# Feature sums by one wide product of ones, in place of token columns and diagonals

## The chip, the core and the metric

The kernel runs on one core of a Trainium2 chip. The metric is the device time of one execution, in microseconds (us). A core has five engines that run their own instruction streams in program order: PE (TensorE, matrix products), DVE (VectorE), ACT (ScalarE), POOL (GpSimd) and SP (SyncE, which only starts transfers here). They wait for each other through semaphores. In profile rows an instruction is given with the line of the kernel that issued it, as L256, and with the tiles it writes and reads, as `mm<-xH,wH`.

## What is computed

Two layers of three sub-layers each act on 512 tokens of 1024 features in float32: a gated feed-forward block (FFN), a mixing block (Mix) and a second FFN. Each sub-layer takes `rmsnorm(x)` over the features, computes its branch, and adds `rmsnorm(branch)` to `x`. Mix holds four branches; one of them, the convolution, ends in a layernorm over 256 features.

```
def rmsnorm(x, g):
    y = x * lax.rsqrt(jnp.mean(x * x, axis=-1, keepdims=True) + EPS)
    return y * g
...
for l in range(DEPTH):
    x = x + 0.5 * rmsnorm(swiglu_ffn(rmsnorm(x, ffn1_pre_g[l]), ...), ffn1_post_g[l])
    x = x + rmsnorm(mixing_sublayer(rmsnorm(x, mix_pre_g[l]), ...), mix_post_g[l])
    x = x + 0.5 * rmsnorm(swiglu_ffn(rmsnorm(x, ffn2_pre_g[l]), ...), ffn2_post_g[l])
```

## The kernel before

Features lie on the 128 partitions and tokens along the row: `x` is 8 tiles of 128x512. Every weight block of 128x1024 is loaded by a transfer (`raw`) and split into a rounded high part `wH` (ACT, L200) and a rest `wL` (DVE, L205, or in places ACT L202 and a transfer that adds on POOL's queue, L203). The activations are split likewise into `xH` (ACT L411) and `xL` (DVE L417). A product is then three matmuls, high by high, high by low and low by high (L256; L290 in the interleaved form `heads`), so PE issues some eleven thousand matmuls. Its results go to 8 banks of the accumulator memory, named by the pools `mm`, `at` and `st`; `st` has two banks.

Two kinds of statistics are on the change's path. They are sums over features, that is over partitions, so PE forms them.

**Before a sub-layer** (`pre_stats`): DVE adds up the squares of `x` (L460) into `sqx`. `compact` multiplies each 128-token block of `sqx` with one column of ones (L317: the block is the stationary operand, the result is one column of tokens), four columns for 512 tokens. DVE takes the inverse square root on this 128x4 tile by small operations without a table (`rsqrt`, L297 to L304), and `diag` (L325) spreads each column over a diagonal 128x128 block. Later `spread` (L333) multiplies ones with the diagonals, which puts each token's value on every partition, and ACT copies it to `rb_` (L365). The sub-layer's products run on unnormalised `x`, since the scale per token can be applied to the result; so only what reads a finished bank (L476 in an FFN, L649 in a Mix) waits for `rb_`.

**After a sub-layer** (`post_stats`, `post_steps`): the same for the branch's output in two token halves of 256 (`lo`, `hi`). The last four of the eight output tiles are computed half by half (`tail`), the statistics of one half run under other products, then for each `k` of 8 DVE scales the output tile (L403, which reads the `spread` bank), DVE or POOL adds it to `x` (L406), ACT makes the next `xH` (L411) and DVE `xL` (L417). The next sub-layer's first four banks (`head`) follow, first for `lo`, then for `hi`; they eat `xH` in the order of `k`. Their end is the compact for the next `pre_stats`, and two more products (`ahead`) come before the first finished bank is needed again.

In Mix the branches are generators that `pump` advances in turn while PE works on gate products; a `yield` gives a cost in ns, and a second number the rounds to sit out. The convolution's layernorm uses compact, diag and spread twice (mean, then variance).

The place of a piece among PE's instructions is set by `after(ns, fn)`, which runs `fn` when an estimate of PE's time has moved on by `ns`:

```
self.after(5600, lambda: nc.scalar.activation(self.rb_, self.spread(dg, FULL), AF.Copy))
...
self.after(3400, lambda: self.step(steps))
```

## Time and profile before

| what | value |
|---|---|
| time, median of 3 runs (lowest to highest) | 2317.3 us (2317.05 to 2317.96) |
| the profiled execution: time, span | 2318.88 us, 2317.2 us |
| PE busy | 2279.9 us, 98% |
| DVE busy | 1195.5 us, 52% |
| ACT busy | 924.4 us, 40% |
| POOL busy | 249.1 us, 11% |

The span reaches from the first to the last instruction of one profiled execution; 1.7 us lie around it. Shares are averages over the whole span, in which long stretches of back-to-back matmuls alternate with the passages from one sub-layer to the next, where DVE, ACT and POOL have a chain of work to finish.

### The profile page before, as it was taken

The numbers are of one execution on the slowest core, as the hardware profiler recorded it, in microseconds if no ns is written. First come the engines' busy times: TensorE is split into PE (matmuls) and PEld (weight loads), VectorE is DVE, ScalarE is ACT, GpSimd is POOL, SyncE is SP. The second block draws the span as 40 slices with busy tenths as digits, with TensorE's granted clock in tenths as the row PEclk, the third lists the DMA queues.
The fourth block names the chain that finished last, engine by engine and source line by source line (L and its number), as shares of the span: only waits on it lengthen the run. The fifth ranks groups of instructions, "written<-read, shape, count | busy, mean of one in ns | idle before, by whom it ended". The sixth has DMA issues, their size and how long they took to land.

```text
span 2317.2 us, 28269 instructions
## 1 busy us (share of the span) xinstructions
PE 2279.9 (98%) x11158; PEld 1907.1 (82%) x11158; DVE 1195.5 (52%) x2144; ACT 924.4 (40%) x1350; POOL 249.1 (11%) x291
## 2 busy tenths in 40 slices
PE   8999999999999999999999999999999999999997
PEld 7888889777888988888888888888787889888886
DVE  5333337799533652434563333478984337424345
ACT  5232224565554532222442222365645545322221
POOL 0000002311431200000100000023123212000001
PEclk9999999999999999999999999999999999999999
DMA  5333333767878432332333333357677774333322
GB/s 171 98 101 92 108 92 99 182 146 168 188 164 184 110 109 91 98 101 90 107 105 97 105 95 102 91 131 162 147 173 162 180 164 109 101 93 94 103 89 69
DMA packets 82557, 282.27 MB, mean 122 GB/s; under 512 B 9428, under 2 KB 13176, under 8 KB 82424
## 3 DMA queue, kind: packets, MB, share of 16 engines
q1 hardware_dynamic: 64136, 213.87, 29.3%
q0 software_dynamic: 18288, 66.59, 16.7%
q8 instruction: 87, 1.43, 0.2%
q14 instruction: 46, 0.38, 0.0%
HBM read 278.32 MB, written 2.10 MB: 121 GB/s over the span
## 4 chain that ended last, share of the span: by engine, by line
PE 87%; DVE 8%; ACT 2%; issue 2%; DMA 1%; POOL 0%; SPq 0%; POOLq 0%; DVEq 0%; ACTq 0%
PE mm L256 49%; PE at L256 31%; DVE ca L868 3%; PE mm L290 2%; PE at L290 2%; DMA wL<-in_w_in_dram 1%; DVE m L937 1%; DVE sc L938 1%; PE st L333 1%; PE st L317 1%; ACT wH L200 1%; ACT wL L202 1%; ACT xH L411 0%; DVE t L649 0%; DVE t L403 0%
## 5 line engine op out<-in xcount | busy, mean ns | idle before, releaser
L200 ACT ACTIVATE wH<-raw 128x1024 fp32r<-128x1024 f32 (+1 forms) x394 | 407.6, 1037 | 828.0 <-issue 570.2
L256 PE MATMUL mm<-xH,wH 128*128 128x512 f32 x1344 | 532.0, 397 | 0.9 <-DVE t L759 0.9
L256 PE MATMUL mm<-xH,wL 128*128 128x512 f32 x1344 | 526.6, 393 | 3.2 <-DMA wL<-in_w_in_dram 3.2
L205 DVE TENSOR_TENSOR wL<-raw,wH 128x1024 fp32r<-128x1024 f32 (+1 forms) x272 | 324.3, 1194 | 247.3 <-ACT wH L200 247.2
L256 PE MATMUL mm<-h,wH 128*128 128x512 f32 (+1 forms) x1496 | 409.1, 354 | 0.0
L256 PE MATMUL mm<-xL,wH 128*128 128x512 f32 x1344 | 359.0, 389 | 0.0
L256 PEld LDWEIGHTS mm<-xH,wL 128*128 128x128 f32 x1344 | 254.2, 189 | 58.5 <-DMA wL<-in_w_in_dram 5.4
L256 PEld LDWEIGHTS mm<-xH,wH 128*128 128x128 f32 x1344 | 254.1, 189 | 57.8 <-issue 5.0
L256 PEld LDWEIGHTS mm<-h,wH 128*128 128x128 f32 x1496 | 263.8, 188 | 41.3
L256 PEld LDWEIGHTS mm<-xL,wH 128*128 128x128 f32 x1344 | 252.3, 188 | 52.5
L256 PE MATMUL at<-xH,wH 128*128 128x512 f32 x704 | 277.4, 396 | 7.3 <-ACT xH L226 6.8
L256 PE MATMUL at<-xH,wL 128*128 128x512 f32 x704 | 274.1, 391 | 0.0
L256 PE MATMUL mm<-h,wL 128*128 128x512 f32 (+1 forms) x748 | 252.4, 352 | 0.0
L256 PE MATMUL at<-h,wH 128*128 128x512 f32 (+1 forms) x776 | 219.6, 366 | 0.0
L202 ACT ACTIVATE wL<-raw 128x1024 fp32r<-128x1024 f32 x122 | 128.4, 1054 | 185.9 <-PE mm L256 129.8
L256 PE MATMUL at<-xL,wH 128*128 128x512 f32 x704 | 187.8, 389 | 0.0
L256 PEld LDWEIGHTS at<-xH,wH 128*128 128x128 f32 x704 | 132.9, 189 | 37.7 <-ACT xH L226 7.1
L256 PEld LDWEIGHTS at<-h,wH 128*128 128x128 f32 x776 | 140.4, 188 | 24.6
L256 PEld LDWEIGHTS mm<-h,wL 128*128 128x128 f32 x748 | 140.4, 188 | 20.3
L256 PEld LDWEIGHTS at<-xH,wL 128*128 128x128 f32 x704 | 132.9, 189 | 29.4 <-issue 1.4
L256 PEld LDWEIGHTS at<-xL,wH 128*128 128x128 f32 x704 | 132.2, 188 | 27.4
L256 PE MATMUL at<-h,wL 128*128 128x512 f32 (+1 forms) x388 | 136.5, 366 | 0.0
(212 smaller groups left out, 2263.4 us busy)
## 6 DMA issues: line engine op xcount, KB each, us to landing
raw<-in_ffn_w_gu_dram SPq DMA_DIRECT2D x173, 512.0 KB, 3.6
raw<-in_w_in_dram SPq DMA_DIRECT2D x98, 512.0 KB, 6.4
wL<-in_w_in_dram POOLq DMA_DIRECT2D x94, 512.0 KB, 7.1
raw<-in_ffn_w_down_dram SPq DMA_DIRECT2D x64, 448.0 KB, 3.3
raw<-in_ffn_w_down_dram SPq DMA_DIRECT2D x32, 512.0 KB, 3.5
raw<-in_w_branch_dram SPq DMA_DIRECT2D x16, 512.0 KB, 5.6
wL<-in_w_branch_dram POOLq DMA_DIRECT2D x16, 512.0 KB, 6.8
raw<-in_w_out_dram SPq DMA_DIRECT2D x16, 512.0 KB, 6.4
```

The costliest lines, as they stand in the source:

```text
L200: self.pin(nc.scalar.activation(h[:, :n], raw[:, :n], AF.Copy))
L202: self.pin(nc.scalar.activation(lo[:, :n], raw[:, :n], AF.Copy, scale=-1.0))
L205: self.pin(nc.vector.tensor_tensor(lo[:, :n], raw[:, :n], h.bitcast(F32)[:, :n], op=ALU.subtract))
L256: self.nc.tensor.matmul(out, w[a], m[b], start=(first and i == 0), stop=(last and i == 3 * n - 1))
L290: self.nc.tensor.matmul(out, w[a], m[b], start=(count[j] == 1), stop=(count[j] == 3 * KD))
L317: self.nc.tensor.matmul(ps[:, c - c0:c - c0 + 1], s[:, c * P:(c + 1) * P], self.ones[:, 0:1], start=(i == 0), stop=(i == len(tiles) - 1))
L333: self.nc.tensor.matmul(ps[:, s], self.ones, dg[:, s], start=True, stop=True)
L868: nc.vector.scalar_tensor_tensor(a, hp[:, t:t + N], dw(t), a, op0=ALU.mult, op1=ALU.add)
L937: nc.vector.max(m8, sc[:, :W])
L938: nc.vector.match_replace(out=sc[:, :W], in_to_replace=m8, in_values=sc[:, :W], imm_value=GONE)
```

## The change

`compact`, `diag` and `spread` go. In their place `sums` multiplies a full 128x128 tile of ones with the squares themselves (L313): one float32 matmul of 512 or 256 columns, whose result holds the token's sum on every partition at once. `rsqrt` then works on 128x512 or 128x256 tiles rather than 128x4 or 128x2, and its result is used from SBUF as it stands; ACT's copy to `rb_` is gone. `ROOT` folds a constant factor into the first operation. In `pre_stats` the sums now stand 2000 ns into `ahead` (before, `compact` ahead of it and `spread` 5600 ns into it). In the convolution each compact-and-spread pair becomes one sums; its yields are changed. In gmlp `rsqrt` keeps its 128x4 tiles and loses one operation.

```diff
-CUBIC = 0.375
+ROOT = 8.0 / 3.0
...
-    def rsqrt(self, y, v, exact=False):
+    def rsqrt(self, y, v, t):
 
         nc = self.nc
-        t, h = self.s8(v.shape[-1]), self.s8(v.shape[-1])
         nc.vector.tensor_scalar(y.bitcast(I32), v.bitcast(I32), -0.5, float(0x5f3759df), op0=ALU.mult, op1=ALU.add)
         nc.vector.tensor_tensor(t, y, y, op=ALU.mult)
         nc.vector.scalar_tensor_tensor(t, t, -0.5, v, op0=ALU.mult, op1=ALU.mult)
         nc.vector.scalar_tensor_tensor(y, t, 1.5, y, op0=ALU.add, op1=ALU.mult)
         nc.vector.tensor_tensor(t, y, y, op=ALU.mult)
-        nc.vector.tensor_tensor(h, t, v, op=ALU.mult)
-        nc.vector.scalar_tensor_tensor(t, h, -10.0 / 3.0, h, op0=ALU.add, op1=ALU.mult)
+        nc.vector.tensor_tensor(t, t, v, op=ALU.mult)
+        nc.vector.scalar_tensor_tensor(t, t, -10.0 / 3.0, t, op0=ALU.add, op1=ALU.mult)
         nc.vector.scalar_tensor_tensor(y, t, 5.0, y, op0=ALU.add, op1=ALU.mult)
-        if exact:
-            nc.vector.tensor_scalar(y, y, CUBIC, None, op0=ALU.mult)
 
     def s8(self, w):
         return self.t([P, 8], F32, "s8", 8)[:, :w]
 
-    def compact(self, tiles, cs):
...
-    def diag(self, r, cs, f=CUBIC):
...
-    def spread(self, dg, cs):
+    def sums(self, tiles, cs):
 
         ps = self.pt("st")
         s = slice(*cs)
-        self.nc.tensor.matmul(ps[:, s], self.ones, dg[:, s], start=True, stop=True)
-        return ps
+        for i, t in enumerate(tiles):
+            self.nc.tensor.matmul(ps[:, s], self.ones, t[:, s], start=(i == 0), stop=(i == len(tiles) - 1))
+        return ps[:, s]
 
 
     def split_x(self, g, cs):
@@ -352,38 +332,38 @@
             self.sq_add(self.sqx, self.xt[k], cs, k == 0)
 
     def pre_stats(self, sub):
+        self.after(2000, lambda: self.pre_root(sub))
+        sub.ahead()
+
+    def pre_root(self, sub):
         nc = self.nc
-        rc = self.s8(4)
-        self.ep = self.t([P, 4], F32, "rc", 2)
+        ps = self.sums([self.sqx], FULL)
+        v, t = self.tmp(), self.tmp()
         self.rb_ = self.t([P, N], F32, "rb_", 1)
-        ps = self.compact([self.sqx], FULL)
-        ms = self.s8(4)
-        nc.vector.tensor_scalar(ms, ps, 1.0 / D, EPS, op0=ALU.mult, op1=ALU.add)
-        self.rsqrt(rc, ms)
-        dg = self.diag(rc, FULL)
-        nc.vector.tensor_scalar(self.ep, ms, EPS, None, op0=ALU.mult)
-        self.after(5600, lambda: nc.scalar.activation(self.rb_, self.spread(dg, FULL), AF.Copy))
-        sub.ahead()
+        nc.vector.tensor_scalar(v, ps, ROOT ** 2 / D, ROOT ** 2 * EPS, op0=ALU.mult, op1=ALU.add)
+        self.rsqrt(self.rb_, v, t)
+        if sub.half:
+            self.ep = self.t([P, N], F32, "ep", 1)
+            nc.vector.tensor_scalar(self.ep, v, 4.0 * EPS, None, op0=ALU.mult)
 
     def post_stats(self, sq, cs, half):
 
 
         nc = self.nc
-        c0 = cs[0] // P
-        ps = self.compact([sq], cs)
-        w = ps.shape[-1]
-        ms, r = self.s8(w), self.s8(w)
+        s = slice(*cs)
+        ps = self.sums(sq, cs)
+        v, t, y = (self.tmp()[:, s] for _ in range(3))
         if half:
-            nc.vector.scalar_tensor_tensor(ms, ps, 1.0 / D, self.ep_prev[:, c0:c0 + w], op0=ALU.mult, op1=ALU.add)
+            nc.vector.scalar_tensor_tensor(v, ps, 4.0 * ROOT ** 2 / D, self.ep_prev[:, s], op0=ALU.mult, op1=ALU.add)
         else:
-            nc.vector.tensor_scalar(ms, ps, 1.0 / D, EPS, op0=ALU.mult, op1=ALU.add)
-        self.rsqrt(r, ms)
-        return self.diag(r, cs, CUBIC * (0.5 if half else 1.0))
+            nc.vector.tensor_scalar(v, ps, ROOT ** 2 / D, ROOT ** 2 * EPS, op0=ALU.mult, op1=ALU.add)
+        self.rsqrt(y, v, t)
+        return y
 
     def post(self, s, cs, nxt):
 
-        dg = self.post_stats(s.sq, cs, s.half)
-        steps = self.post_steps(s, cs, nxt, dg)
+        y = self.post_stats([s.sq], cs, s.half)
+        steps = self.post_steps(s, cs, nxt, y)
         self.after(3400, lambda: self.step(steps))
 
     def step(self, steps):
@@ -391,16 +371,15 @@
         if ns is not None:
             self.after(ns, lambda: self.step(steps))
 
-    def post_steps(self, s, cs, nxt, dg):
+    def post_steps(self, s, cs, nxt, y):
         nc = self.nc
         c = slice(*cs)
         first = cs == HALVES[0]
-        pb = self.spread(dg, cs)
         if first and nxt:
             self.new_x()
         for k in range(KD):
             u = self.tmp()
-            nc.vector.scalar_tensor_tensor(u[:, c], s.o[k][:, c], self.v(s.post[0], s.post[1] + k), pb[:, c],
+            nc.vector.scalar_tensor_tensor(u[:, c], s.o[k][:, c], self.v(s.post[0], s.post[1] + k), y,
                                            op0=ALU.mult, op1=ALU.mult)
             e = nc.gpsimd if k % 2 and not (first and nxt) else nc.vector
             e.tensor_tensor(self.xt[k][:, c], self.xt[k][:, c], u[:, c], op=ALU.add)
@@ -822,8 +801,8 @@
             vt.append(g)
         yield 0, 1
         ms, r = b.s8(4), b.s8(4)
-        nc.vector.tensor_scalar(ms, ssq, 1.0 / C, EPS, op0=ALU.mult, op1=ALU.add)
-        b.rsqrt(r, ms, True)
+        nc.vector.tensor_scalar(ms, ssq, ROOT ** 2 / C, ROOT ** 2 * EPS, op0=ALU.mult, op1=ALU.add)
+        b.rsqrt(r, ms, b.s8(4))
         yield 1000
         vn = []
         for cp in range(2):
@@ -872,30 +851,23 @@
         both = b.tmp()
         nc.gpsimd.tensor_tensor(both, acc[0], acc[1], op=ALU.add)
         yield 0, 1
-        ps = b.compact([both], FULL)
-        mu = b.s8(4)
-        nc.vector.tensor_scalar(mu, ps, 1.0 / C, None, op0=ALU.mult)
-        dg = b.diag(mu, FULL, 1.0)
-        yield 500, 1
-        pb = b.spread(dg, FULL)
+        ps = b.sums([both], FULL)
         sq = []
         for j in range(2):
-            nc.vector.tensor_tensor(acc[j], acc[j], pb, op=ALU.subtract)
+            nc.vector.scalar_tensor_tensor(acc[j], ps, -1.0 / C, acc[j], op0=ALU.mult, op1=ALU.add)
             q = b.tmp()
             nc.scalar.activation(q, acc[j], AF.Square)
             sq.append(q)
         nc.gpsimd.tensor_tensor(sq[0], sq[0], sq[1], op=ALU.add)
-        yield 1200, 1
-        ps = b.compact([sq[0]], FULL)
-        ms, r = b.s8(4), b.s8(4)
-        nc.vector.tensor_scalar(ms, ps, 1.0 / C, EPS, op0=ALU.mult, op1=ALU.add)
-        b.rsqrt(r, ms)
-        dg = b.diag(r, FULL)
-        yield 1500, 1
-        pb = b.spread(dg, FULL)
+        yield 1400, 1
+        ps = b.sums([sq[0]], FULL)
+        r, ms, t = b.tmp(), b.tmp(), b.tmp()
+        nc.vector.tensor_scalar(ms, ps, ROOT ** 2 / C, ROOT ** 2 * EPS, op0=ALU.mult, op1=ALU.add)
+        b.rsqrt(r, ms, t)
+        yield 5200
         self.b3 = []
         for j in range(2):
-            nc.vector.tensor_tensor(acc[j], acc[j], pb, op=ALU.mult)
+            nc.vector.tensor_tensor(acc[j], acc[j], r, op=ALU.mult)
             nc.vector.tensor_scalar(acc[j], acc[j], self.ln2[:, j:j + 1], self.ln2[:, 2 + j:3 + j],
                                     op0=ALU.mult, op1=ALU.add)
             th = b.tmp()
```

The lines of the changed program that the text names: L313 sums; L343 the first operation of a pre chain, L357 that of an FFN's post chain, both reading the `st` bank; L296 to L303 rsqrt; L347 `ep`; L382, L385, L390, L396 what L403, L406, L411, L417 were; L439 what L460 was; L455 what L476 was; L739 and L959 what L760 and L987 were.

How the order on the engines moves, at three places. First DVE at the passage from the first FFN to the first Mix, second half: from the statistics to the first scaling of an output tile. `s` are the small tiles, `st` the accumulator bank, `t` a 128x512 temporary, `y` the output tiles. Before:

```order
L377 SCALAR_TENSOR_TENSOR s_501_2759<-st_2756,rc_272 128x2
L297 TENSOR_SCALAR s_502_2760<-s_501_2759 128x2
L298 TENSOR_TENSOR s_503_2762<-s_502_2760 128x2
L299 SCALAR_TENSOR_TENSOR s_503_2762<-s_503_2762,s_501_2759 128x2
L300 SCALAR_TENSOR_TENSOR s_502_2760<-s_503_2762,s_502_2760 128x2
L301 TENSOR_TENSOR s_503_2762<-s_502_2760 128x2
L302 TENSOR_TENSOR s_504_2763<-s_503_2762,s_501_2759 128x2
L303 SCALAR_TENSOR_TENSOR s_503_2762<-s_504_2763 128x2
L304 SCALAR_TENSOR_TENSOR s_502_2760<-s_503_2762,s_502_2760 128x2
L325 TENSOR_SCALAR t_2772<-ident,s_502_2760 128x128 x2
L205 TENSOR_TENSOR wL_2797<-raw_2794,wH_2796 128x1024
L403 SCALAR_TENSOR_TENSOR t_2815<-y_769,vec,st_2813 128x256
```

Now:

```order
L357 SCALAR_TENSOR_TENSOR t_2738<-st_2736,ep_303 128x256
L296 TENSOR_SCALAR t_2740<-t_2738 128x256
L297 TENSOR_TENSOR t_2739<-t_2740 128x256
L298 SCALAR_TENSOR_TENSOR t_2739<-t_2739,t_2738 128x256
L299 SCALAR_TENSOR_TENSOR t_2740<-t_2739,t_2740 128x256
L300 TENSOR_TENSOR t_2739<-t_2740 128x256
L301 TENSOR_TENSOR t_2739<-t_2739,t_2738 128x256
L302 SCALAR_TENSOR_TENSOR t_2739<-t_2739 128x256
L303 SCALAR_TENSOR_TENSOR t_2740<-t_2739,t_2740 128x256
L205 TENSOR_TENSOR wL_2772<-raw_2769,wH_2771 128x1024
L382 SCALAR_TENSOR_TENSOR t_2788<-y_756,vec,t_2740 128x256
L382 SCALAR_TENSOR_TENSOR t_2798<-y_789,vec,t_2740 128x256
```

The nine small operations and the two diagonal blocks have become nine operations on 256 columns, still one after the other; the weight split L205 and the scaling come behind them as before.

Second, DVE at the start of the second FFN of layer 1, where `rb_` is formed while the weights of `ahead` and of the third block are split. Before, from the second operation behind the weight split to the first reader of `rb_`:

```order
L364 TENSOR_SCALAR rc_6823<-s_1318_6830 128x4
L298 TENSOR_TENSOR s_1319_6832<-s_1314_6822 128x4
L299 SCALAR_TENSOR_TENSOR s_1319_6832<-s_1319_6832,s_1318_6830 128x4
L300 SCALAR_TENSOR_TENSOR s_1314_6822<-s_1319_6832,s_1314_6822 128x4
L301 TENSOR_TENSOR s_1319_6832<-s_1314_6822 128x4
L302 TENSOR_TENSOR s_1320_6833<-s_1319_6832,s_1318_6830 128x4
L303 SCALAR_TENSOR_TENSOR s_1319_6832<-s_1320_6833 128x4
L304 SCALAR_TENSOR_TENSOR s_1314_6822<-s_1319_6832,s_1314_6822 128x4
L325 TENSOR_SCALAR t_6842<-ident,s_1314_6822 128x128 x4
L205 TENSOR_TENSOR wL_6943<-raw_6940,wH_6942 128x1024
L205 TENSOR_TENSOR wL_7008<-raw_7005,wH_7007 128x1024
L476 TENSOR_TENSOR t_6907<-at_6536,rb__1316_6824 128x512
```

Now, from the second wide operation (the first, L343, stands just ahead) to the same reader, L455:

```order
L296 TENSOR_SCALAR rb__1295_6763<-t_6761 128x512
L347 TENSOR_SCALAR ep_6773<-t_6761 128x512
L297 TENSOR_TENSOR t_6762<-rb__1295_6763 128x512
L298 SCALAR_TENSOR_TENSOR t_6762<-t_6762,t_6761 128x512
L205 TENSOR_TENSOR wL_6849<-raw_6846,wH_6848 128x1024
L299 SCALAR_TENSOR_TENSOR rb__1295_6763<-t_6762,rb__1295_6763 128x512
L205 TENSOR_TENSOR wL_6914<-raw_6911,wH_6913 128x1024
L300 TENSOR_TENSOR t_6762<-rb__1295_6763 128x512
L301 TENSOR_TENSOR t_6762<-t_6762,t_6761 128x512
L302 SCALAR_TENSOR_TENSOR t_6762<-t_6762 128x512
L303 SCALAR_TENSOR_TENSOR rb__1295_6763<-t_6762,rb__1295_6763 128x512
L455 TENSOR_TENSOR t_6813<-at_6462,rb__1295_6763 128x512
```

Two L205 that stood between the chain (and its diagonals) and the reader now stand among the wide operations.

Third, ACT in the first Mix, among the weight splits for the gate products. Before:

```order
L223 ACTIVATE y_4184<-t_4057 128x512
L223 ACTIVATE y_4191<-t_4066 128x512
L200 ACTIVATE wH_4346<-raw_4344 128x1024
L760 ACTIVATE t_4227<-t_4227 128x512
L202 ACTIVATE wL_4347<-raw_4344 128x1024
L987 ACTIVATE h_3371<-at_4170 64x128
L200 ACTIVATE wH_4422<-raw_4420 128x1024
```

Now:

```order
L223 ACTIVATE y_4140<-t_4015 128x512
L223 ACTIVATE y_4147<-t_4024 128x512
L202 ACTIVATE wL_4303<-raw_4300 128x1024
L200 ACTIVATE wH_4302<-raw_4300 128x1024
L739 ACTIVATE t_4183<-t_4183 128x512
L959 ACTIVATE h_3329<-at_4126 64x128
L200 ACTIVATE wH_4378<-raw_4376 128x1024
```

The L202 that starts the low part of the weight shown last before (`wL_4347`, now `wL_4303`) stood behind L200 and L760 and now stands ahead of both.

## Rows read from the trace of the kernel before

**Rows 1.** Page, busy time of each engine (share of the span) and instructions.
```profile
PE 2279.9 (98%) x11158; PEld 1907.1 (82%) x11158; DVE 1195.5 (52%) x2144; ACT 924.4 (40%) x1350; POOL 249.1 (11%) x291
```

**Rows 2.** Page, the chain that ended last: share by engine, then by line.
```profile
PE 87%; DVE 8%; ACT 2%; issue 2%; DMA 1%; POOL 0%; SPq 0%; POOLq 0%; DVEq 0%; ACTq 0%
PE mm L256 49%; PE at L256 31%; DVE ca L868 3%; PE mm L290 2%; PE at L290 2%; DMA wL<-in_w_in_dram 1%; DVE m L937 1%; DVE sc L938 1%; PE st L333 1%; PE st L317 1%; ACT wH L200 1%; ACT wL L202 1%; ACT xH L411 0%; DVE t L649 0%; DVE t L403 0%
```

**Rows 3.** Waits of PE: who waited for whom, us in total, times, longest.
```profile
PE at L256 <- DVE t L224: 8.0, 2, 4.1
PE mm L256 <- DMA wL<-in_w_in_dram: 3.2, 2, 1.8
PE st L317 <- DVE t L460: 2.8, 1, 2.8
PE st L333 <- DVE t L325: 2.3, 1, 2.3
PE at L290 <- ACT xH L411: 1.1, 3, 0.4
```

**Rows 4.** Timeline of PE, opening of the third sub-layer: start, duration, instruction, count.
```profile
811.94 0.95 PE L317 MATMUL st<-ones,t 128*128 128x1 f32 x8
812.75 0.47 PE L256 MATMUL mm<-xH,wH 128*128 128x512 f32 x1
813.07 0.39 PE L256 MATMUL mm<-xH,wL 128*128 128x512 f32 x1
...
818.77 1.02 PE L333 MATMUL st<-t,ones 128*128 128x512 f32 x2
819.23 0.80 PE L256 MATMUL at<-xH,wH 128*128 128x512 f32 x1
819.87 0.40 PE L256 MATMUL at<-xH,wL 128*128 128x512 f32 x1
...
824.67 0.39 PE L256 MATMUL at<-xH,wH 128*128 128x512 f32 x1
```

**Rows 5.** Groups by line and shape on DVE: busy us, mean ns, idle before.
```profile
L868 DVE SCALAR_TENSOR_TENSOR ca<-cv,vec,ca 128x512 f32<-128x512 f32 x120 | 92.5, 794 | 0.2
...
L403 DVE SCALAR_TENSOR_TENSOR t<-y,vec,st 128x256 f32<-128x256 f32 x96 | 41.8, 474 | 11.0 <-PE st L333 10.9
L460 DVE TENSOR_TENSOR t<-t,t 128x512 f32<-128x512 f32 x60 | 41.3, 689 | 35.9 <-ACT t L458 32.0
...
L460 DVE TENSOR_TENSOR t<-t,t 128x256 f32<-128x256 f32 x30 | 13.3, 442 | 20.4 <-ACT t L458 20.4
```

**Rows 6.** Timeline of DVE, first FFN to first Mix: [idle before, releaser].
```profile
368.04 0.16 DVE L377 SCALAR_TENSOR_TENSOR s<-st,rc 128x2 f32<-128x2 f32 x1 [0.70 <-PE st L317]
...
372.00 0.48 DVE L403 SCALAR_TENSOR_TENSOR t<-y,vec,st 128x256 f32<-128x256 f32 x1 [1.50 <-PE st L333]
...
382.61 0.14 DVE L377 SCALAR_TENSOR_TENSOR s<-st,rc 128x2 f32<-128x2 f32 x1
...
384.36 0.48 DVE L325 TENSOR_SCALAR t<-ident,s 128x128 f32<-128x128 f32 x2
384.76 1.22 DVE L205 TENSOR_TENSOR wL<-raw,wH 128x1024 fp32r<-128x1024 f32 x1
385.95 0.88 DVE L403 SCALAR_TENSOR_TENSOR t<-y,vec,st 128x256 f32<-128x256 f32 x2
```

**Rows 7.** Timeline of ACT and PE in the same passage, second half.
```profile
391.36 0.90 ACT L411 ACTIVATE xH<-x,vec 128x256 fp32r<-128x256 f32 x2
...
393.21 0.28 PE L290 MATMUL at<-xH,h 128*128 128x256 f32 x1
```

**Rows 8.** Timeline of PE and DVE, the end of the kernel.
```profile
2304.53 0.58 PE L317 MATMUL st<-ones,t 128*128 128x1 f32 x4 [2.75 <-DVE t L460]
2305.14 0.16 DVE L377 SCALAR_TENSOR_TENSOR s<-st,rc 128x2 f32<-128x2 f32 x1 [0.76 <-PE st L317]
...
2307.44 1.22 PE L333 MATMUL st<-t,ones 128*128 128x256 f32 x2 [2.34 <-DVE t L325]
2308.70 0.87 DVE L403 SCALAR_TENSOR_TENSOR t<-y,vec,st 128x256 f32<-128x256 f32 x2 [1.31 <-PE st L333]
```

13 lines of the change are left out of this document (removed).

## Prediction

> **What bounds the kernel now.** I read the page first. PE is busy for 2279.9 of 2317.2 us, DVE for half the span [rows 1], and the chain that ended last is PE for 87% of it, nearly all of it in the big products L256; the two lines that the change takes off PE's order, L317 and L333, hold about 1% each [rows 2]. So PE sets the end almost everywhere, and what the change is worth has two parts: slots that it frees on PE's stream, and places where PE would have to wait for DVE. For the second I read PE's waits: they name few places [rows 3], and none of them is the opening of a sub-layer. Then I read the timelines of three places where the statistics stand: an opening [rows 4], a passage between sub-layers [rows 6, 7] and the end [rows 8].
>
> **What PE gains.** A slot is read from start to start. In the opening, `compact` starts at 811.94, one main product follows at 812.75 and the next at 813.07 [rows 4]. Main products start about 0.23 us apart when nothing else stands there, so the four small column products cost 1.13 - 0.23 = 0.90 us. `spread` costs 819.87 - 818.77 - 0.23 = 0.87 us in the same way, and the new `sums` is the same instruction as a spread, float32 with 512 columns, and should cost the same 0.87. A half (two columns, or 256 columns) I take at half of that, 0.45 and 0.43. A spread goes for each sums that comes, so what is gained is one compact for each pair: 6 openings x 0.90 = 5.4; 5 passages x 2 halves x 0.45 = 4.5; in each convolution two compacts, 2 x 2 x 0.90 = 3.6; together 13.5 us, 0.6%. The Trainium skill, Perfetto Trace Analysis, section Engine Utilization, judges a kernel by the engine that nears full utilization; taken by that alone, with PE at 98%, all 13.5 us would be saved.
>
> **What DVE loses.** A chain on 128x2 tiles starts at 382.61 and its nine operations and two diagonal blocks end at 384.36 + 0.48 = 384.84, 2.2 us later; each operation costs (384.36 - 382.61) / 9 = 0.19 us [rows 6]. No row shows a wide rsqrt, so I price its kinds by the nearest rows: scalar_tensor_tensor 0.47 and tensor_tensor 0.44 on 256 columns, 0.79 and 0.69 on 512 [rows 5]; the tensor_scalar I put below both, 0.3 and 0.55. Each operation waits for the one before it. The small ones leave no more than 0.03 us between them, which is the value I use; the rows on L460, whose operations also wait for ACT, allow about 0.1. A half chain (five scalar_tensor_tensor with the first, three tensor_tensor, one tensor_scalar, eight gaps) is 2.35 + 1.33 + 0.3 + 0.25 = 4.2 us. A full chain of an FFN's opening with `ep` is 3 x 0.55 + 3 x 0.69 + 4 x 0.79 + 0.25 = 7.1, of a Mix's opening 6.5. The bounds: 3.8 and 6.5 (overlapping operations) below, 5.0 and 8 (0.1 between them) above.
>
> **Passages FFN to Mix (three).** In the first half the scaling L403 starts at 372.00, 3.96 us after the chain did, of which 1.50 were a wait for the spread [rows 6]. That cover takes up the longer chain except for some 0.65 us: 4.2, and an addition of 0.42 that DVE now does at another place. From there to the second half DVE has no idle time, so the second chain starts 0.65 late. It is 4.2 instead of 2.2 long, the weight split of 1.22 stands behind it as before, and the spread that L403 waited for before was already there; so L403's successor starts 0.65 + 2.0 = 2.65 us late. Next late are the `xH` of the second half. The last pair before starts at 391.36 and ends at 392.26; PE first needs the last at about 393.2 [rows 7], a margin of 0.95. So PE gets it at 392.26 + 2.65 = 394.9, that is 1.7 us later than it does now, whatever it saved before that place: the 0.9 saved in the passage is spent waiting. **+1.7 each, +5.1.** The existing short waits of PE for this ACT line, 1.1 us in three [rows 3], are of the same kind and show how near the edge it is.
>
> **Passages Mix to FFN (two).** Here DVE stands idle ahead of the second chain and the `xH` have over 2 us of margin. The 2.0 us of the longer chain use it up, little is left of the saving: **-0.1 each, -0.2.**
>
> **FFN openings.** From the compact's place, T0 = 811.94, PE next needs a bank that only L476 frees at 824.67, T0 + 12.7 [rows 4]; with the compact gone it comes at T0 + 11.8. The sums stand ten products in, end at T0 + 2.3 + 0.87, the chain of 7.1 follows with two L205 of 1.2 among it, and the reader takes 0.69: T0 + 13.3. PE waits 1.5, less the 0.9 saved: about **+0.5 each for three of them, +1.5**. At the kernel's first opening the order has one such L205, not two, in the chain: **-0.4.** In the Mix openings the chain is shorter, without `ep`, and DVE has nothing else in it; between nothing and the whole 0.9 I keep **-0.3 each, -0.6.**
>
> **Convolutions.** PE has no wait around them, and the wide chain runs in the background under gate products, so the saving is kept: **-3.6.** **The Mix's order.** Two weights come late for PE, 3.2 us in two waits, the longer 1.8 [rows 3]. In the first Mix the L202 that starts such a late weight moves ahead of an L200 and an L760, which is worth its 1.4: **-1.4.** In the second Mix the order on POOL's queue shifts too; I leave it at 0 with -4 to +3 around it. The two long waits for L224 (8.0) stay as they are, since what stands ahead of them is the attention's own chain.
>
> **The end.** Here nothing covers DVE. The chain from L377 at 2305.14 to L403 at 2308.70 is 3.56 us, with 1.22 of spread in it [rows 8]; now it is 4.2 with no spread, +0.65; the sums may take 0.6 to 1.2 us where the compact took 0.58, +0.2; and DVE's first half comes 0.6 late: **+1.4.**
>
> **Sum.** 5.1 - 0.2 + 1.5 - 0.4 - 0.6 - 3.6 - 1.4 + 1.4 = +1.8 us, 2318.9 + 1.8 = 2320.7 for the profiled execution; that one lies 1.6 above the median of the runs, so 2317.3 + 1.8 = 2319.1 for the median. I say 2319.
>
> **Rivals.**
> - *Faster: the chains fit.* Say a wide operation costs 0.33, half way between the small one's 0.19 and 0.47. The half chain is then 3.0, the `xH` of the second half come 0.8 late, inside their margin of 0.95, so the three passages give -0.1 each instead of +1.7 (-5.4), the two others keep their 0.9 (-1.6), and the four FFN openings keep theirs (-0.9 each instead of +1.1 together, -4.7): 1.8 - 11.7 = -9.9, 2307. Half of that shortening gives about 2313. For it: PE waits for none of this today beyond tenths. Against it: the means of three groups of 30 to 120 instructions [rows 5]. The Trainium skill's VectorE: DVE Perf Modes says that a float32 operation on two tensors runs at one element per cycle of 0.96 GHz; its Perfetto Trace Analysis, section Optimizing Scalar/DVE Operations, adds some 60 ns for each; by these pages 256 columns are an estimated 0.33 us; the trace disagrees, with 0.44 and 0.47 [rows 5]. Chance 0.27.
> - *Slower: the gap between dependent wide operations is 0.1 us, not 0.03.* Then a half chain is 0.6 longer, both halves 1.2: three passages +3.6, the two others lose their margin, +2.4, three FFN openings of ten operations +2.1: 1.8 + 8.1 = 9.9, 2327. It decides from a gap of about 0.06 up, where the sum passes +4.6. For it: every operation of the chain reads the result of the one before it. Against it: so do the small ones, 0.19 us apart. Chance 0.18.
> - *The Mix's order decides.* A new late weight or a late last attention step, at the upper bound: +3 and up, 2322 and more: 0.05. At the lower bound (-4) the time stays within what can be told from no change.
>
> The forecast has the remaining 0.5. A measurement of this kernel tells about 0.2%, 4.6 us, from no change: so faster 0.27, the same 0.50, slower 0.23. The range takes in most of both rivals, 2308 to 2328; for my own case alone it is 2313 to 2322.
>
> **What would show it.** In the changed trace: L313 with 512 columns in slots of 0.87; half chains L357 to L303 of 4.2 us; PE at L290 waiting for the new L390 by 1 to 2 us in each of three passages, and for none in the two others; a wait of 1 to 2 us in three FFN openings for the reader L455; no wait around the convolutions; the end of the kernel longer by a little over 1 us. I am wrong if half chains come out at 3 us (then the rival above it), if PE waits for L390 by more than 2.5, or if PE's waits inside the Mixes change by more than 4 us.

## The result, and the profile after

The changed kernel takes 2333.51 us in the median against 2317.63 for the kernel before; the ratio is 1.0066, with a 95% interval from 1.0053 to 1.008. It is slower by 0.5 to 0.8%. The forecast was 2319 us with 2308 to 2328 around it, so the time lies above the range. The profiled execution has a span of 2330.9 us, 13.7 more than before.

The page of the changed kernel, busy times and the chain that ended last, against [rows 1] and [rows 2]:

```profile
PE 2271.5 (97%) x11030; PEld 1898.0 (81%) x11030; DVE 1256.3 (54%) x2074; ACT 925.9 (40%) x1346; POOL 252.3 (11%) x291
...
PE 80%; DVE 13%; issue 2%; ACT 2%; DMA 2%; POOL 0%; SPq 0%; POOLq 0%; ACTq 0%; DVEq 0%
PE mm L256 47%; PE at L256 30%; DVE sc L910 1%; DVE ca L847 1%; DVE t L382 1%; DVE m L909 1%; PE at L290 1%; PE mm L290 1%; DMA raw<-in_ffn_w_gu_dram 1%; ACT wH L200 1%; DVE wL L205 1%; DVE x L385 1%; PE st L313 1%; ACT xH L390 0%; DVE t L300 0%
```

PE has 8.4 us less to do than before, and its share of the last chain falls from 87% to 80%, while DVE's rises from 8% to 13%. The freed slots are there; PE now waits. Who PE waits for in the changed kernel, against [rows 3] (us in total, times, longest):

```profile
PE at L256 <- DVE t L224: 7.5, 2, 3.8
PE at L256 <- ACT xH L226: 7.1, 1, 7.1
PE at L290 <- ACT xH L390: 6.6, 16, 1.0
PE mm L256 <- DMA wL<-in_w_in_dram: 6.5, 1, 6.5
PE st L313 <- DVE t L439: 4.7, 1, 4.7
PE mm L290 <- ACT wH L200: 4.5, 5, 1.1
PE at L256 <- DVE t L455: 4.4, 3, 1.8
```

The two long waits for L224 are the old ones, and so is that for L226 in the first FFN, 6.8 us before, which [rows 3] leaves out. New are the waits of the four opening banks (L290) for `xH` and for weights, 6.6 and 4.5 us where there were 1.1 and none; one wait of 6.5 us for a weight's low part; three for the reader of `rb_`, L455; and 4.7 instead of 2.8 at the last statistics.

The passage from the first FFN to the first Mix, second half, against [rows 6] and [rows 7]; the timeline of DVE, POOL and ACT (start, duration, instruction, count), with one scaling of the first half ahead of it:

```profile
372.72 1.50 DVE L382 SCALAR_TENSOR_TENSOR t<-y,vec,t 128x256 f32<-128x256 f32 x2
...
373.02 0.91 POOL L439 TENSOR_TENSOR t<-t,t 128x256 f32<-128x256 f32 x1
...
383.84 0.41 DVE L357 SCALAR_TENSOR_TENSOR t<-st,ep 128x256 f32<-128x256 f32 x1
...
387.37 0.42 DVE L303 SCALAR_TENSOR_TENSOR t<-t,t 128x256 f32<-128x256 f32 x1
387.71 1.22 DVE L205 TENSOR_TENSOR wL<-raw,wH 128x1024 fp32r<-128x1024 f32 x1
388.85 0.87 DVE L382 SCALAR_TENSOR_TENSOR t<-y,vec,t 128x256 f32<-128x256 f32 x2
389.64 0.42 DVE L385 TENSOR_TENSOR x<-x,t 128x256 f32<-128x256 f32 x1
389.82 0.84 POOL L385 TENSOR_TENSOR x<-x,t 128x256 f32<-128x256 f32 x1 [9.21 <-DVE t L382]
389.98 1.36 DVE L382 SCALAR_TENSOR_TENSOR t<-y,vec,t 128x256 f32<-128x256 f32 x2
...
391.41 0.85 POOL L385 TENSOR_TENSOR x<-x,t 128x256 f32<-128x256 f32 x1 [0.76 <-DVE t L382]
391.59 1.34 DVE L382 SCALAR_TENSOR_TENSOR t<-y,vec,t 128x256 f32<-128x256 f32 x2
...
395.24 0.89 ACT L390 ACTIVATE xH<-x,vec 128x256 fp32r<-128x256 f32 x2
```

The chain runs from 383.84 to 387.79, 3.95 us; 4.2 were forecast. What was not forecast comes behind it: the first pair of scalings takes 0.87 us, as before, but the next ones, which run beside an add of POOL, take 1.36 and 1.34. Read one by one, it is the scaling that starts beside the add that is slow:

```profile
389.98 0.96 DVE L382 SCALAR_TENSOR_TENSOR t<-y,vec,t 128x256 f32<-128x256 f32 x1
390.86 0.47 DVE L382 SCALAR_TENSOR_TENSOR t<-y,vec,t 128x256 f32<-128x256 f32 x1
```

The first half has the same beside POOL's adds of squares (L439): 1.50 for a pair. The last `xH` starts at 395.24, 3.9 us later than before, and 2.65 were forecast. Over the whole program the group of the scaling reads, where L403 had a mean of 474 ns [rows 5]:

```profile
L382 DVE SCALAR_TENSOR_TENSOR t<-y,vec,t 128x256 f32<-128x256 f32 x96 | 55.0, 612 | 0.2
```

To see where the 13.7 us arise I compare the two traces at the same products: the first and the last product of the four opening banks of each passage (the 192 rows of L290 there). Differences to the kernel before, in us, in each stretch, one number for each stretch named:

```
stretch                              after   forecast
passages out of an FFN (three)       +3.8 +3.6 +3.7    +1.7 each
passages Mix to FFN (two)            +2.2 +2.2         -0.1 each
FFN openings and bodies (four)       -0.6 -0.1 -0.9 -0.9    -0.4 +0.5 +0.5 +0.5
first Mix, second Mix                +4.5 -8.4         -5.6 together
end, from PE's last branch product   +4.5              +1.4
```

They add up to +13.7. The three passages out of an FFN are those that the forecast calls FFN to Mix; one of them leads to the next FFN. The stretches do not hold quite the same work: in each of these three the changed kernel has two main products (L256) that stood outside it before. At 0.23 us each, the three are at +3.4 +3.2 +3.2 for equal products. PE's clock has no part in the passages: the granted clock is 1.00 in all five, before and after.

At the FFN's opening the finished banks are read as forecast: the chain ends at 834.88 and L455 reads at 834.92, 1.5 us late on the mean of three waits.

```profile
825.29 0.69 DVE L343 TENSOR_SCALAR t<-st 128x512 f32<-128x512 f32 x1 [0.90 <-PE st L313]
...
834.19 0.69 DVE L303 SCALAR_TENSOR_TENSOR rb__1295_6763<-t,rb__1295_6763 128x512 f32<-128x512 f32 x1
834.92 0.69 DVE L455 TENSOR_TENSOR t<-at,rb__1295_6763 128x512 f32<-128x512 f32 x1
```

The end, against [rows 8]:

```profile
2315.70 1.22 PE L313 MATMUL st<-t,ones 128*128 128x256 f32 x2 [4.72 <-DVE t L439]
2316.96 0.42 DVE L357 SCALAR_TENSOR_TENSOR t<-st,ep 128x256 f32<-128x256 f32 x1 [1.32 <-PE st L313]
...
2320.96 0.88 DVE L382 SCALAR_TENSOR_TENSOR t<-y,vec,t 128x256 f32<-128x256 f32 x2
...
2325.29 1.33 DVE L382 SCALAR_TENSOR_TENSOR t<-y,vec,t 128x256 f32<-128x256 f32 x2
```

From the sums to the last scaling it is 2325.29 - 2315.70 = 9.6 us; in the first of four pairs, 0.88, POOL has no add yet, and in the last, 1.33, it has.

### The profile page after: what moved, and what is told of

Same layout as the page of the kernel before. It is cut to its first block, busy times and chain, and to the rows that moved or that the text cites. A ratio compares the mean times of both kernels' runs of the same rounds, so it can differ in the third digit from the quotient of the medians.

```text
span 2330.9 us, 27933 instructions
## 1 busy us (share of the span) xinstructions
PE 2271.5 (97%) x11030; PEld 1898.0 (81%) x11030; DVE 1256.3 (54%) x2074; ACT 925.9 (40%) x1346; POOL 252.3 (11%) x291
## 4 chain that ended last, share of the span: by engine, by line
PE 80%; DVE 13%; issue 2%; ACT 2%; DMA 2%; POOL 0%; SPq 0%; POOLq 0%; ACTq 0%; DVEq 0%
PE mm L256 47%; PE at L256 30%; DVE sc L910 1%; DVE ca L847 1%; DVE t L382 1%; DVE m L909 1%; PE at L290 1%; PE mm L290 1%; DMA raw<-in_ffn_w_gu_dram 1%; ACT wH L200 1%; DVE wL L205 1%; DVE x L385 1%; PE st L313 1%; ACT xH L390 0%; DVE t L300 0%
## 5 line engine op out<-in xcount | busy, mean ns | idle before, releaser
L200 ACT ACTIVATE wH<-raw 128x1024 fp32r<-128x1024 f32 (+1 forms) x394 | 407.3, 1038 | 824.7 <-issue 562.0
L256 PE MATMUL mm<-xH,wH 128*128 128x512 f32 x1344 | 534.9, 399 | 1.6 <-DVE t L738 1.6
L256 PE MATMUL mm<-xH,wL 128*128 128x512 f32 x1344 | 527.7, 394 | 6.6 <-DMA wL<-in_w_in_dram 6.5
L205 DVE TENSOR_TENSOR wL<-raw,wH 128x1024 fp32r<-128x1024 f32 (+1 forms) x272 | 323.9, 1194 | 239.2 <-ACT wH L200 239.0
L256 PE MATMUL mm<-h,wH 128*128 128x512 f32 (+1 forms) x1496 | 406.4, 352 | 0.0
L256 PE MATMUL mm<-xL,wH 128*128 128x512 f32 x1344 | 359.2, 389 | 0.0
L256 PEld LDWEIGHTS mm<-xH,wL 128*128 128x128 f32 x1344 | 255.0, 190 | 63.4 <-DMA wL<-in_w_in_dram 8.4
L256 PEld LDWEIGHTS mm<-xH,wH 128*128 128x128 f32 x1344 | 254.8, 190 | 59.2 <-issue 6.8
L256 PEld LDWEIGHTS mm<-h,wH 128*128 128x128 f32 x1496 | 265.1, 189 | 38.2
L256 PEld LDWEIGHTS mm<-xL,wH 128*128 128x128 f32 x1344 | 252.3, 188 | 52.7
L256 PE MATMUL at<-xH,wH 128*128 128x512 f32 x704 | 275.5, 393 | 12.4 <-ACT xH L226 7.1
L256 PE MATMUL at<-xH,wL 128*128 128x512 f32 x704 | 274.4, 392 | 0.0
L256 PE MATMUL mm<-h,wL 128*128 128x512 f32 (+1 forms) x748 | 252.6, 352 | 0.0
L256 PE MATMUL at<-h,wH 128*128 128x512 f32 (+1 forms) x776 | 218.7, 365 | 0.0
L202 ACT ACTIVATE wL<-raw 128x1024 fp32r<-128x1024 f32 x122 | 128.4, 1053 | 175.1 <-PE mm L256 143.6
L256 PE MATMUL at<-xL,wH 128*128 128x512 f32 x704 | 187.8, 389 | 0.0
L256 PEld LDWEIGHTS at<-xH,wH 128*128 128x128 f32 x704 | 133.2, 189 | 42.6 <-ACT xH L226 7.4
L256 PEld LDWEIGHTS at<-h,wH 128*128 128x128 f32 x776 | 140.9, 189 | 23.4
L256 PEld LDWEIGHTS mm<-h,wL 128*128 128x128 f32 x748 | 141.5, 189 | 19.1
L256 PEld LDWEIGHTS at<-xH,wL 128*128 128x128 f32 x704 | 133.2, 189 | 27.9 <-DVE wL L205 0.3
L256 PEld LDWEIGHTS at<-xL,wH 128*128 128x128 f32 x704 | 132.2, 188 | 27.5
L256 PE MATMUL at<-h,wL 128*128 128x512 f32 (+1 forms) x388 | 136.5, 365 | 0.7 <-DMA wL<-in_w_out_dram 0.7
```

Source lines behind the costliest of these rows:

```text
L200: self.pin(nc.scalar.activation(h[:, :n], raw[:, :n], AF.Copy))
L202: self.pin(nc.scalar.activation(lo[:, :n], raw[:, :n], AF.Copy, scale=-1.0))
L205: self.pin(nc.vector.tensor_tensor(lo[:, :n], raw[:, :n], h.bitcast(F32)[:, :n], op=ALU.subtract))
L256: self.nc.tensor.matmul(out, w[a], m[b], start=(first and i == 0), stop=(last and i == 3 * n - 1))
```

## The experiments

Times are medians (of one run where no ratio is given), ratios are those to the kernel before on the same chip, with their 95% intervals. The segments are those of the table above, against the kernel before. A segment moves somewhat by itself: the first FFN stands at +0.6 to +1.6 and the passages out of an FFN at up to +1.2 in runs below in which nothing of them was changed.

**The factor back in the accumulator.** In the changed kernel the last rsqrt operation of a post chain writes `pb`:

```diff
     def post_stats(self, sq, cs, half):
...
-        self.rsqrt(y, v, t)
-        return y
+        pb = self.pt("st")[:, s]
+        self.rsqrt(y, v, t, pb)
+        return pb
```

> The changed kernel, with one difference: the last of the eight rsqrt operations of a post chain writes its result to an accumulator bank (st), so that the scaling L382 reads the factor from there, as L403 did, and not from SBUF. Theory A (the scaling with both tiles in SBUF is slowed by POOL's adds running beside it): the scaling falls back from a mean of 0.61 us to 0.47, its pairs in the second half stand 1.12 apart instead of 1.61, each of the five passages gets about 1.4 us shorter and the end about 1.5: 2324 to 2326 us. Theory B (only the longer chain of wide operations counts): the scaling stays as it is, 2332 to 2335 us.

Measured: 2322.7 us, ratio 1.001 (0.9999 to 1.0021), 11 us less than the changed kernel. The group of the scaling in this run:

```profile
L383 DVE SCALAR_TENSOR_TENSOR t<-y,vec,st 128x256 f32<-128x256 f32 x96 | 41.6, 475 | 0.2
```

The second pair of the passage shown above, beside POOL's add:

```profile
388.42 0.82 POOL L386 TENSOR_TENSOR x<-x,t 128x256 f32<-128x256 f32 x1 [9.23 <-DVE t L383]
388.57 0.87 DVE L383 SCALAR_TENSOR_TENSOR t<-y,vec,st 128x256 f32<-128x256 f32 x2
```

The passages are at +2.6 +0.8 +2.4 +2.5 +0.2, 7.0 us less than in the changed kernel, and the rest of the program with the end 3.0 less. Theory A holds, and somewhat more strongly than its number: of the 13.7 us in the spans 10.0 go with the place of one operand. These passages hold three main products more than before (one in the two from Mix to FFN); for equal products they are at +1.9 +0.6 +1.7 +1.8 0.0, and the forecast was +1.7 and -0.1.

**The other way round: the kernel before with its factor in SBUF** (`pbs` is a tile of ones).

```diff
-        pb = self.spread(dg, cs)
+        pp = self.spread(dg, cs)
+        pb = self.pbs
+        nc.vector.tensor_copy(pb[:, cs[0]:cs[0] + 1], pp[:, cs[0]:cs[0] + 1])
```

> The kernel before, with one difference: the scaling L403 reads its factor from a tile in SBUF, into which one column of the spread's bank is copied, so that it waits for the same spread as before; the factor is a constant otherwise, so the output is not the reference's. The chains stay small. Theory A: the scaling beside POOL's adds takes up to twice as long, its pairs stand 1.6 apart; the margins of 0.95 and 2 us in the passages hide most of it, the end shows it whole: +0.5 for each of three passages, 0 to 0.5 for two, +1.5 at the end, so 2320 to 2322 us. Theory B: no change, 2317 to 2318 us.

Measured: 2326.64 us, ratio 1.0037 (1.0024 to 1.0049). All five passages, the first FFN's body and the end grow (+1.7 +0.1 +1.3 +1.4 +0.1, +1.4, +2.9), with nothing changed in the chains but a copy of one column:

```profile
L407 DVE SCALAR_TENSOR_TENSOR t<-y,vec,pbs 128x256 f32<-128x256 f32 x96 | 54.1, 603 | 0.3
```

The direction is theory A's and the size is larger than expected. At the end the first half pays too: PE's wait ahead of the last statistics is 4.0 us instead of 2.8. The first FFN's +1.4 is no more than it shows where nothing of it was changed, so it is not shown to belong to the operand.

With the kernels before and after, the two runs give the four cases of short or long chain and fast or slowed scaling. Out of an FFN the prices add, for equal products: about +1.5 for the slowed scaling alone, +1.8 for the long chain with the rest of the change, +3.3 for both. From Mix to FFN neither alone costs more than 0.6, and both cost 2.2: there each fits into the margin, and the two together do not.

**All adds on DVE, none on POOL** (changed kernel, factor still in SBUF):

```diff
-            e = nc.gpsimd if k % 2 and not (first and nxt) else nc.vector
+            e = nc.vector
```

> The changed kernel with all adds of the passages (L385) on DVE, none on POOL; the scaling still reads its factor from SBUF. If it is POOL's work beside it that slows the scaling, it falls to 0.47 us each in the second half although both its tiles are in SBUF; a pair with its two adds then takes 0.87 + 0.75 = 1.5 us against 1.61 now, so the passages get a few tenths shorter: 2331 to 2334 us. If two tiles in SBUF are slow by themselves, the scaling stays above 0.6 us and the passages get 1 us longer each, 2338 or more.

Measured: 2331.3 us in one run. The group, then DVE's scalings and POOL's work in the first passage:

```profile
L382 DVE SCALAR_TENSOR_TENSOR t<-y,vec,t 128x256 f32<-128x256 f32 x96 | 45.9, 518 | 0.2
```

```profile
372.38 1.51 DVE L382 SCALAR_TENSOR_TENSOR t<-y,vec,t 128x256 f32<-128x256 f32 x2
...
377.08 1.34 DVE L382 SCALAR_TENSOR_TENSOR t<-y,vec,t 128x256 f32<-128x256 f32 x2
...
379.01 0.87 DVE L382 SCALAR_TENSOR_TENSOR t<-y,vec,t 128x256 f32<-128x256 f32 x2
...
389.99 0.88 DVE L382 SCALAR_TENSOR_TENSOR t<-y,vec,t 128x256 f32<-128x256 f32 x2
```

```profile
372.69 0.92 POOL L439 TENSOR_TENSOR t<-t,t 128x256 f32<-128x256 f32 x1
...
377.38 0.75 POOL L439 TENSOR_TENSOR t<-t,t 128x256 f32<-128x256 f32 x1 [0.48 <-ACT t L437]
379.42 0.86 POOL L203 DMA_DIRECT2D wL<-in_w_in_dram  x1 [1.29 <-ACT wL L202]
```

In the second half, 389.99, POOL does nothing and a pair takes 0.88, both tiles in SBUF. In the first half the pairs beside POOL's adds of squares (L439 at 372.69 and 377.38) still take 1.51 and 1.34, while the pair at 379.01, beside the start of a transfer on POOL (L203), takes 0.87. So it is POOL's work beside it, not the place of the tile alone. The passages do get shorter, by more than expected: for equal products (nine main products more than before in the passages out of an FFN, five in the others) they are at +1.5 +0.7 +1.3 +1.4 +0.7, 8.6 us less than in the changed kernel, although DVE now has all the adds. The first Mix, the third FFN and the second Mix are 4.1, 2.5 and 1.8 us longer than there, counted in the same way; no run separates why.

**A shorter chain** (changed kernel, four of the eight operations left out in the post chains):

```diff
+        if short:
+            return
         nc.vector.tensor_tensor(t, y, y, op=ALU.mult)
```

> The changed kernel, with the second step of rsqrt (four of its eight wide operations) left out in the post chains only, so the factor is less exact. It asks what an operation of the chain costs in time: a half chain gets 4 x 0.46 = 1.84 us shorter. If the chain lies on the path: 1.5 to 2.5 us less in each of five passages and 1.8 at the end, about 2321 to 2325 us. If the chain is covered and only the slowed scaling counts: less than 3 us in all, 2330 to 2333.

Measured: 2315.22 us in one run, 18 us less and below the expected 2321 to 2325. The passages fall to +0.2 -0.5 +1.0 +0.9 -0.5, by 2.2 to 3.1 each for equal products, and the last FFN with the end from +3.6 to +0.1. The chain is on the path too. An operation that is left out of both halves of a passage takes 0.6 to 0.8 us off it, more than the 0.46 of one half, since both halves shorten. One of the four was itself slowed by POOL in the changed kernel: in the first half after each FFN L300 runs beside L439 and takes 0.85, which raises its mean to 566 ns where L299 has 425.

```profile
L300 DVE TENSOR_TENSOR t<-t 128x256 f32<-128x256 f32 x12 | 6.8, 566 | 0.4
L299 DVE SCALAR_TENSOR_TENSOR t<-t,t 128x256 f32<-128x256 f32 x12 | 5.1, 425 | 0.4
```

Either remedy alone takes most of the loss away: chain and slowed scaling use up the same margin.

**Token columns after a sub-layer** (changed kernel; compact, diag and spread for the post statistics, `ep` added to the squares ahead of them):

```diff
                 if last:
                     b.sq_add(self.sq, self.o[d], FULL, d == 0)
+                    if d == 0:
+                        nc.vector.scalar_tensor_tensor(self.sq, b.ep, D / P, self.sq, op0=ALU.mult, op1=ALU.add)
```

> The changed kernel, with the statistics after a sub-layer taken back to token columns, diagonals and spread (compact, diag, spread as before); the openings and the convolution keep the wide form. The wide ep is added to the squares by one DVE operation in the body of an FFN. If the passages and the end are where the change loses (15.5 us in five passages and 4.5 at the end, by the two traces), they come back: 2311 to 2316 us. If DVE's load in the openings or the Mixes is what makes the passages longer, they stay: 2325 or more.

Measured: 2315.91 us, ratio 0.9988 (0.9979 to 0.9998). All passages are within 0.2 us of before, the end too, and the three later FFNs gain 0.5 to 0.7 each. The Mixes stand at +6.3 and -7.0: they have nothing to do with the passages.

**Which part moves the Mixes.** Four runs: the changed kernel with the old convolution; the kernel before with the new one; and two on the run with token columns, one with only the convolution's mean in the wide form, one with the whole old convolution, which leaves the wide openings alone. The edit from new to old convolution, of which the second is the reverse and the third a part:

```diff
-        ps = b.sums([both], FULL)
+        ps = b.compact([both], FULL)
...
-        b.rsqrt(r, ms, t)
-        yield 5200
...
+        b.rsqrt_c(r, ms)
+        dg = b.diag(r, FULL)
+        yield 1500, 1
```

> The changed kernel with the convolution's layernorm of before (compact, diag and spread, small rsqrt, the old yields); openings and post chains stay wide. Theory C (the wide rsqrt of the convolution, 6 us of DVE, holds up ACT's queue and with it a weight split, so that PE waits some 7 us for a weight in the first Mix; the same change of order takes stalls out of the second Mix): the first Mix comes back from +4.5 to within 1 us of before, the second from -8.4 to between -2 and 0; in all 2333 to 2338 us, with the 3.6 us of product slots back. Theory D (the earlier products after the openings shift the Mixes): the first keeps +4.5 or more and the second -5 or less.

Measured: 2331.91 us, ratio 1.0058 (1.0042 to 1.0074); Mixes at -2.2 and -2.8. The first Mix comes back, somewhat further than theory C said, and no wait for a weight's low part above 1.0 is left; theory D is out. The second keeps a little more of its gain than expected.

> The kernel before with the changed kernel's convolution alone (two sums, wide rsqrt, new yields). Theory C: the first Mix 4 to 7 us longer by one wait for a weight, the second 6 to 9 shorter; passages and openings as before; 2313 to 2319 us. Theory D: both Mixes 1.8 us shorter by the freed product slots and no new wait of PE, 2313 to 2315 us with the first Mix at -1.8.

Measured: 2323.23 us, ratio 1.0017 (1.0006 to 1.0027); Mixes at +8.1 and -5.6, slower than either theory's sum; the wait of theory C is there. In this kernel's first Mix, PE's waits, then ACT and POOL ahead of the late weight (L917 is the convolution's tanh, L224 a split of its result, L201 and L203 the weight's split, L793 an add to the gated sum, L204 the weight's transfer):

```profile
PE mm L257 <- DMA wL<-in_w_in_dram: 8.5, 3, 7.3
```

```profile
617.62 0.63 ACT L917 ACTIVATE t<-ca 128x512 f32<-128x512 f32 x1 [1.75 <-DVE ca L914]
...
620.81 0.63 ACT L224 ACTIVATE h<-t 128x512 fp32r<-128x512 f32 x1 [2.26 <-DVE t L918]
...
623.08 1.05 ACT L201 ACTIVATE wH<-raw 128x1024 fp32r<-128x1024 f32 x1
...
625.58 1.04 ACT L203 ACTIVATE wL<-raw 128x1024 fp32r<-128x1024 f32 x1
```

```profile
625.96 1.68 POOL L793 TENSOR_TENSOR y<-y,t 128x512 f32<-128x512 f32 x1 [6.07 <-DVE t L791]
627.57 0.87 POOL L204 DMA_DIRECT2D wL<-in_w_in_dram  x1
```

ACT waits 1.75 and 2.26 us for the convolution's results on DVE, and the weight's split stands behind them, in two pieces; on POOL its transfer stands behind an add that has waited 6.07. It starts at 627.57.

The late weight costs more than the wait. While PE stands still, from 629.0 to 636.2, the granted clock falls, and it rises only behind 641.9. Two stretches behind the wait (length; busy time and instructions of PE, PEld, DVE, ACT, POOL; granted clock; DMA share, GB/s), and two products in the first:

```profile
636.20:641.90 5.70, 5.68 (x13) 4.45 (x14) 0.00 (x0) 0.00 (x0) 0.00 (x0) 0.50 0.92 229
641.90:647.60 5.70, 5.70 (x30) 4.80 (x29) 1.46 (x3) 2.91 (x4) 0.85 (x1) 0.99 0.12 9
```

```profile
641.08 0.63 PE L257 MATMUL mm<-xH,wH 128*128 128x512 f32 x1
641.50 0.63 PE L257 MATMUL mm<-xH,wL 128*128 128x512 f32 x1
```

At 0.50, which is 1.2 GHz, products start 0.43 us apart instead of 0.23, so the 13 of them take 2.8 us more. Neither theory had that in its sum. In the second Mix the reverse happens: the kernel before has a late weight there, 1.79 us, with the clock at 0.50 for the products behind it, and with the new convolution that wait is gone.

> As the run with token columns after a sub-layer (wide openings, wide convolution), but in the convolution only the mean is a wide sums; the variance goes back to compact, small rsqrt, diag and spread, so DVE's 6 us of wide rsqrt are gone there. Theory C: the late weight of the first Mix (8 us) goes, 2308 to 2313 us, if the second Mix keeps its gain; 2314 to 2318 if that goes too. Theory D: as that run, 2315 to 2317.

Measured: 2316.72 us, ratio 0.9986 (0.9976 to 0.9997); Mixes at +0.6 and -0.8: the late weight has gone (no wait for one above 2.6), and the second Mix's gain with it. The time alone would also fit theory D; the Mixes do not.

> As the run with token columns after a sub-layer, with the old convolution too: of the change only the wide openings are left (and gmlp's one operation less). By that run's trace an opening's FFN gains 0.5 to 0.9 us: 2314 to 2317 us with both Mixes within 1 us of before if theory C holds; by theory D the first Mix stays some 6 us longer and the second some 7 shorter.

Measured: 2312.7 us, ratio 0.9969 (0.9957 to 0.998); Mixes at -2.2 and -3.2, three FFNs at -0.6 to -0.8. Both Mixes gain more than the 1 us that theory C allowed, and the time is below the expected range; theory D is out again. This is the best of the kernels here: the wide openings alone are faster than both.

**What in the new convolution makes the weight late.** The kernel before with the new convolution, its rsqrt on 4 columns of a constant tile:

```diff
-        b.rsqrt_w(r, ms, t)
+        b.rsqrt_w(r[:, :4], ms[:, :4], t[:, :4])
```

> The run with the new convolution alone, but its eight rsqrt operations work on 4 columns of a constant tile instead of 512, so the output is not the reference's; sums, yields and everything on PE are the same. If the wide operations on DVE (6 us) make the weight late, with the order on ACT and POOL that goes with them, the first Mix has no wait above 3 us and falls from +8.1 to +2 or less: 2312 to 2318 us. If the changed yields and the product order do it, the wait of some 7 us stays, 2321 or more.

Measured: 2312.87 us in one run; Mixes at -1.1 and -6.0, no wait for a weight's low part above 0.7 us and one of 1.3 for a high part. So the width of the rsqrt makes it, with the order on ACT and POOL that follows from it, and not the yields or the products: PE's order is the same in both runs, and on ACT the weight's split now stands ahead of the convolution's second tanh.

**The splits kept in written order** (kernel before with the new convolution):

```diff
+        b.pinned = True
         yield 5200
...
             yield 2300
+        b.pinned = False
```

> The run with the new convolution alone, where the weight splits that are issued while the convolution's last part is open keep the order in which they are written on ACT and DVE, instead of being put behind the convolution's and the attention's steps. If the weight is late because its split stands behind those steps on ACT and behind an add on POOL, the wait of 7 us in the first Mix goes or falls below 3: 2313 to 2318 us. If the transfer itself is late for another reason, it stays at 2321 or more.

Measured: 2375.78 us in one run, Mixes at +23 and +31, with seven waits for weights (30 us). Wrong by far: with this order both Mixes are much longer. It does not tell which of the two made the weight late, DVE's time or the place of the split on ACT; that stays open.

**Earlier sums** (wide openings only):

```diff
-        self.after(2000, lambda: self.pre_root(sub))
+        self.after(200, lambda: self.pre_root(sub))
```

> The run with wide openings only, with the sums of an opening 200 ns into the two products instead of 2000, so the wide chain starts some 1.8 us earlier. PE's waits for the first reader of rb_ in three FFN openings (2.4 us in all) should go, and the openings gain 0.8 us each: 2309 to 2312 us. If the sums then wait for the squares on DVE, PE stands still there instead and nothing is gained: 2312 to 2315.

Measured: 2313.78 us, ratio 0.998 (0.997 to 0.9989). The three waits for the reader of `rb_` fall from 2.4 to 0.6 us and the FFNs gain another 0.4 to 0.7 each, as expected, and the first Mix 1.6, but a passage and the second Mix give most of it back (+0.9 and +2.2 against the run with the wide openings alone). The time misses the 2309 to 2312 us; it falls into the other range without that one's reason, as no new wait of PE for the squares appears. Not better.

## Why the prediction was wrong

**What PE gains** is borne out in sign and order: PE's busy time falls by 8.4 us (13.5 were forecast, in slots from start to start), and where nothing else happens the time falls: -0.6 to -0.8 for each later FFN and -2.2 and -3.2 for the Mixes with wide openings alone.

**The chain's price** held: 3.95 us for a half chain against 4.2, with 0.42 for an operation on 256 columns and 0.04 between them, where POOL does not work beside it. The slower rival (0.1 between dependent operations) did not happen, so its price decided nothing. The estimate of 0.33 us that the forecast holds against the trace is no profiled duration: the Trainium skill, Perfetto Trace Analysis, section Optimizing Scalar/DVE Operations, calls its 60 ns engine-busy time and says that the profiled latency is about twice that. Scalings in a row started 0.40 us apart in the kernel before (385.95 and 386.35).

**The step that failed is in the passages: "L403's successor starts 0.65 + 2.0 = 2.65 us late. Next late are the xH of the second half."** The working keeps every operation between and behind the chains at its old duration. But the change also moves the factor of the scaling from an accumulator bank to SBUF, and the forecast has no term for that. The scaling becomes an operation with two SBUF tiles, and the one that starts beside an add of POOL takes 0.95 us instead of 0.48. In the second half three such pairs stand ahead of the last `xH`, 0.49 us each; 1.0 of these 1.5 us reach it, so it comes 3.9 late, and the rest goes where it waited for ACT's own queue before. In the first half two stand beside L439, so the second chain starts 1.23 us late (383.84 against 382.61) instead of 0.65. That the scaling behind it starts 2.9 us late (388.85 against 385.95), close to the 2.65, is in part luck, since the second chain is 1.7 longer instead of 2.0. The late `xH` of the first half on ACT also put the next weight split back, the new waits of 4.5 us for L200, which fall to 0.8 with the factor in the accumulator.

So the three passages cost 3.2 to 3.4 us for equal products instead of 1.7, and with the factor in the accumulator 1.7 to 1.9: what the forecast priced came out, and what it left out is the operand. The kernel before showed where this would happen (L403 reads `st`, L406 runs on both engines, and the diff puts `y` in the place of `pb`), and it showed the price as well. There L417, of the same form with two SBUF tiles, starts beside POOL's last add and takes 0.97, where the ones behind it take 0.47:

```profile
390.26 0.85 POOL L406 TENSOR_TENSOR x<-x,t 128x256 f32<-128x256 f32 x1 [0.27 <-DVE t L403]
```

```profile
390.43 0.97 DVE L417 SCALAR_TENSOR_TENSOR xL<-x,vec,xH 128x256 fp32r<-128x256 f32 x1
```

The Trainium skill, SBUF — State Buffer, section Who interferes with whom, states the rule: a VectorE instruction with two SBUF inputs contends with a GpSimd instruction that reads SBUF, and one with at most one SBUF input, outside the modes that use both ports, does not. The traces agree with both halves of it: 1.36 us for a pair beside POOL's add, and 0.87 with POOL idle or with the factor in the accumulator.

**Passages Mix to FFN** failed by the same step, +2.2 instead of -0.1: the margin of 2 us is used up by the chain, and the slowed scaling comes on top. With the factor in the accumulator they are at +0.6 and 0.0 for equal products.

**FFN openings**: the wait was right (1.5 forecast, 4.4 in three measured), but the saving that was set against it was too small; the three gain 0.1 to 0.9 instead of losing 0.5. With wide openings alone these FFNs gain 2.2 in all beside 2.4 of waits, so PE saves about 1.5 in an opening, not 0.9. Where the rest of it comes from no run shows.

**Convolutions**, -3.6 "since the wide chain runs in the background": wrong. It runs on DVE's queue between work that ACT and POOL wait for, and with it come a wait of 7 us for a weight in the first Mix, with products at half the clock behind it, and the loss of a smaller one in the second; the new convolution alone is +2.5 in the two Mixes together, and -7.1 when its rsqrt works on 4 columns. **The Mix's order**: what the L202 that I gave -1.4 is worth no run separates; the Mixes by openings alone gain 5.4, where -0.6 was forecast for their openings. As a sum, -3.8 against the forecast -5.6, the two errors nearly meet, by chance.

**The end**: +4.5 against +1.4. The chain, with no spread in it, is 0.4 longer (0.65 forecast). The sums came out at the upper price, 1.22, which makes 0.65 where 0.2 was put. DVE's first half runs slowed beside POOL, so PE waits 4.7 instead of 2.8, 2.0 more where 0.6 was put, and three slowed pairs add 1.5.

Of the rivals, none had the mechanism that decided. In numbers: of the 11.9 us between the forecast +1.8 and +13.7, the passages make 9.2 for equal products and the end 3.1, and the rest of the program gives 0.4 back.
